# Hard-max attention on one core: dots of four query tiles per operation, and another order of the last gathers and the branch

## The chip, the core and the metric

The kernel runs on one core of one Trainium2 chip. The core has five engines that run their own instruction streams and meet at semaphores: TensorE (PE, with its weight loads as PEld), VectorE (DVE), ScalarE (ACT), GpSimd (POOL) and SyncE (SP). The metric is the device time of one execution in microseconds. Before the change it is 467.06 us, the median of three runs (467.06 to 469.16). The profile is one further execution, of 467.3 us, and its span, from the first to the last instruction, is 465.5 us.

## The reference

Attention in which the softmax is replaced by a hard maximum: every query takes the value row of the one key with the largest dot product. There are 4 batches of 4096 queries and 4096 keys, with 128 elements a row, all in fp32.

```python
def reference(q, k, v):
    logits = np.matmul(q, k.transpose(0, 2, 1))
    best = np.argmax(logits, axis=-1)
    b_idx = np.arange(q.shape[0])[:, None]
    return v[b_idx, best, :].astype(np.float32)
```

## The kernel before

**Tiles and the screen.** The queries form 128 tiles of 128, 32 a batch; `T` is 128. A tile is first screened in low precision. The 4096 keys of a batch are held as 1024 groups of 4 in a form (`kT`) from which the maximum over a group can be had by sums, differences and absolute values. For each tile, PE multiplies queries with that (`mm`, L193) and adds on the absolute values that ACT made (L202, A; added at L212). ACT evicts one half with a Relu to E (L215), DVE folds the other half from PSUM with E into packed words W (`fold`, L228), each of which also carries the number of its group, and a MAX8 takes the eight best groups of the tile (`top`, L232, into TOP).

**Candidates.** `gather` takes the best group's number out of TOP (L244, `cand`) and queues one indirect DMA for each tile, which brings three key differences of 128 elements of each query's group into a buffer `kg` (L250, issued by POOL). Before the change this is done for pairs of tiles, with eight buffers. `dots` then multiplies them with the queries on DVE (L265, `prod`), adds halves twice (L269, L272), and reduces the rest to a number (L274, `D`), again a pair at a time. `pick` compares these for chunks of eight tiles (four near the end) and forms the index of the winning key (L284 to L297: mx, near, sel, CNT, win). `put_values` queues the value gathers by that index (L304, `vr`, one a tile), and a store of four tiles on SP (L309).

**Doubtful rows.** Queries whose screen was too close to call are flagged and done exactly. This is done in two halves of the tiles. The first half is a generator (`flag_segment`) whose steps are spread over the loop's later iterations; its gathers pass through the list `fast`. The second half comes after the loop: `flags_first` and `flags_last`. There DVE and PE pack the doubtful rows' numbers together, POOL gathers their records FR, queries FQ and three candidate groups FK (`get`, L498), `exact` (L542) computes the exact products, the winners' value rows FV are gathered, and one indirect DMA scatters them to the output (L534). If there were more doubtful rows than fit, a count HARD is above zero, and `all_rows` (L571 to L593) redoes everything: all engines read that count (`hi`, L573) and branch over the block (L576). In this data the block is not entered.

**Order.** The kernel writes out the order of every engine's instructions by hand (`manual_schedule`): what is emitted first stands first in its engine's queue. The main loop (L700) runs over 128 iterations `it`. In each it emits, in this order: at most one load (`load_part`, on POOL, for a later batch), at most one piece of the transposed keys of a later batch (`unit_k`: PE, and an ACT eviction, L173), the screen of tile `it`, the fold of tile it-1, one call of `step`, MAX8 of tile it-2, the candidates of tile it-3 (`gathers`; it-2 from iteration 104 on), a second call of `step`, and `issue`. `step` lets each started generator (`dots`, `pick`, flags) go on by one piece of DVE work, with one or two `dots` pieces a call. `issue` puts key gathers (`near_q`) and value gathers (`late_q`) into POOL's queue, one of each per iteration as a rule, and two key gathers from iteration 100 on when more than two are queued. A `dots` generator waits until its gathers are in POOL's queue, then two iterations more (one from iteration 104, `TAIL`). In `yield "until", condition, n` the n is this number of iterations.

**After the loop.** The last tiles' MAX8, candidates and gathers are emitted, then the remaining `dots` and `pick`. `flags_last` mixes its steps with the value gathers that are still queued: `late(n)` emits n of them (L501: `LATE`, 8; L504: one; L525: three; L528: all that are left).

Of the kernel before, what the change touches and what calls it, by code (L numbers as in the profile page):

```python
# [10 lines left out]
U32 = mybir.dt.uint32  # L11
# [9 lines left out]
QSCALE = 128.0  # L21
TAU = 8.0
NEAR = 0.5
LATE = 8


@with_exitstack
def kernel(ctx, tc, q, k, v, out):
# [210 lines left out]
    def gather(c, t0, n):  # L239
        c0, c1 = chunks[c]  # L240
        if t0 == c0:
            cand_t[c] = sp.tile([P, c1 - c0], U32, tag=f"cand{c1 - c0}", name=f"cand_{c}", bufs=6)
        x = cand_t[c][:, t0 - c0:t0 - c0 + n]
        nc.vector.tensor_scalar(out=x, in0=TOP.bitcast(U32)[:, t0:t0 + n, 0], scalar1=IDX, scalar2=IDX,  # L244
                                op0=OP.bitwise_and, op1=OP.bitwise_xor)
        kg = rp.tile([P, n, 3, P], FP16, tag=f"kg{n}", name=f"kg_{t0}", bufs=8)
        assert len(kg_t) < 8
        kg_t[t0] = kg
        for j in range(n):
            near_q.append(lambda j=j: nc.gpsimd.indirect_dma_start(  # L250
                out=kg[:, j].rearrange("p f d -> p (f d)"), out_offset=None, in_=k16[t0 // NQT],
                in_offset=IOA(ap=x[:, j:j + 1], axis=0)))
        mark = lambda: done.add(("kg", t0))
        marks.add(mark)
        near_q.append(mark)
        start(dots(c, t0, n), "dots", c)

    def dots(c, x, m):
        c0 = chunks[c][0]
        d = D_t[c % 4]  # L260
        b = x // NQT
        yield "until", lambda: ("kg", x) in done, 1 if x >= TAIL else 2
        kg = kg_t.pop(x)
        prod = rp.tile([P, m, 3, P], FP16, tag=f"prod{m}", name=f"prod_{x}")
        nc.vector.tensor_tensor(out=prod, in0=kg, in1=natq[b % 2][:, x - b * NQT:x - b * NQT + m, :].unsqueeze(2).to_broadcast([P, m, 3, P]),  # L265
                                op=OP.mult)
        yield "dve",
        p1 = rp.tile([P, m, 3, 64], FP16, tag=f"p1{m}", name=f"p1_{x}")
        nc.vector.tensor_tensor(out=p1, in0=prod[:, :, :, 0:64], in1=prod[:, :, :, 64:128], op=OP.add)  # L269
        yield "dve",  # L270
        p2 = rp.tile([P, m, 3, 32], FP16, tag=f"p2{m}", name=f"p2_{x}")
        nc.vector.tensor_tensor(out=p2, in0=p1[:, :, :, 0:32], in1=p1[:, :, :, 32:64], op=OP.add)  # L272
        yield "dve",
        nc.vector.tensor_reduce(out=d[:, x - c0:x - c0 + m, 1:4], in_=p2, axis=AX_X, op=OP.add)  # L274
        done.add(("dot", x))

    def pick(c, t0, t1):
        n = t1 - t0
        b, qt = t0 // NQT, t0 % NQT
        d = D_t[c % 4][:, 0:n, :]  # L280
        yield "until", lambda: all(("dot", x) in done for x in range(t0, t1, 2)), 0
        cand = cand_t.pop(c)
        mx = sp.tile([P, n, 1], FP32, tag=f"mx{n}", name=f"mx_{c}")
        nc.vector.tensor_reduce(out=mx[:, :, 0], in_=d, axis=AX_X, op=OP.max)  # L284
        yield "dve",
        near = sp.tile([P, n, 4], FP32, tag=f"near{n}", name=f"near_{c}")
        nc.vector.scalar_tensor_tensor(out=near, in0=d, scalar=NEAR, in1=mx.to_broadcast([P, n, 4]),
                                       op0=OP.add, op1=OP.is_ge)
        yield "dve",
        sel = sp.tile([P, n, 4], FP32, tag=f"sel{n}", name=f"sel_{c}")  # L290
        nc.vector.tensor_tensor(out=sel, in0=near, in1=iota8.unsqueeze(1).to_broadcast([P, n, 4]), op=OP.mult)
        yield "dve",
        nc.vector.tensor_reduce(out=CNT[:, t0:t1], in_=sel, axis=AX_X, op=OP.add)
        done.add(("cnt", c))
        yield "cnt",
        win = sp.tile([P, n], U32, tag=f"win{n}", name=f"win_{c}")
        nc.vector.scalar_tensor_tensor(out=win, in0=CNT[:, t0:t1], scalar=float(b * Sk - 8), in1=cand, op0=OP.add, op1=OP.add)  # L297
        for i in range(0, n, 4):
            put_values(c, i, n, win, out[b].rearrange("(p t) d -> p t d", p=P)[:, qt + i:qt + i + 4])
# [151 lines left out]
    def flags_last(t0, t1, win_last, late):  # L451
# [45 lines left out]
        def get(dst, src, idx, hi):  # L497
            nc.gpsimd.indirect_dma_start(out=dst, out_offset=None, in_=src, in_offset=IOA(ap=idx, axis=0),  # L498
                                         bounds_check=hi - 1, oob_is_err=False)
# [22 lines left out]
        nc.vector.tensor_tensor(out=hd[:, 1:2], in0=tot[:, 1:2], in1=tot[:, 0:1], op=OP.subtract)  # L522
        for a in (hd[:, 0:1], hd[:, 1:2], tot[:, 2:3]):
            nc.vector.tensor_tensor(out=HARD, in0=HARD, in1=a, op=OP.add)
        late(3)  # L525
        win = whole(exact(FK, FQ, gb, 3, "fe"))
        get(FV, v_flat, win, B * Sk)
        late(1 << 20)  # L528
        ok = fp.tile([P, 1], FP32, tag="ok", name="ok_e")
        nc.vector.tensor_scalar(out=ok, in0=HARD, scalar1=0.5, scalar2=float(1 << 20), op0=OP.is_gt, op1=OP.mult)  # L530
        rowk = fp.tile([P, 1], U32, tag="rowk", name="rowk_e")
        nc.vector.tensor_tensor(out=rowk, in0=row, in1=ok, op=OP.add)
        all_rows()
        nc.gpsimd.indirect_dma_start(out=out_flat, out_offset=IOA(ap=rowk, axis=0), in_=FV, in_offset=None,  # L534
                                     bounds_check=P * T - 1, oob_is_err=False)

    def exact(kk, qq, grp, R, name):
        d = fp.tile([P, R, 4], FP32, tag=f"xd{R}", name=f"xd_{name}")
        for r in range(R):
            for f in range(4):  # L540
                pr = fp.tile([P, P], FP32, tag="xp", name=f"xp_{name}_{r}_{f}", bufs=2)
                nc.vector.tensor_tensor_reduce(out=pr, in0=kk[:, r, f * P:(f + 1) * P], in1=qq, scale=1.0, scalar=0.0,  # L542
                                               op0=OP.mult, op1=OP.add, accum_out=d[:, r, f:f + 1])
                yield "dve", 0.2
        ix = fp.tile([P, R, 4], FP32, tag=f"xi{R}", name=f"xi_{name}")
        nc.vector.scalar_tensor_tensor(out=ix, in0=grp.unsqueeze(2).to_broadcast([P, R, 4]), scalar=0.0,
                                       in1=iota4.unsqueeze(1).to_broadcast([P, R, 4]), op0=OP.add, op1=OP.add)
        yield "dve", 0.17
        mx = fp.tile([P, 1], FP32, tag="xm", name=f"xm_{name}")
        nc.vector.tensor_reduce(out=mx, in_=d.rearrange("p r f -> p (r f)"), axis=AX_X, op=OP.max)  # L550
        yield "dve", 0.17
        lt = fp.tile([P, R * 4], FP32, tag=f"xl{R}", name=f"xl_{name}")
        nc.vector.tensor_scalar(out=lt, in0=d.rearrange("p r f -> p (r f)"), scalar1=mx, scalar2=float(1 << 20),
                                op0=OP.is_lt, op1=OP.mult)
        yield "dve", 0.17
        nc.vector.tensor_tensor(out=lt, in0=lt, in1=ix.rearrange("p r f -> p (r f)"), op=OP.add)
        yield "dve", 0.17
        win = fp.tile([P, 1], U32, tag="xw", name=f"xw_{name}")
        nc.vector.tensor_reduce(out=win, in_=lt, axis=AX_X, op=OP.min)
        yield "dve", 0.17  # L560
        return win


    def whole(g):
        while True:
            try:
                next(g)
            except StopIteration as s:
                return s.value

    def all_rows():  # L571
        hi = fp.tile([1, 1], mybir.dt.int32, tag="hi")
        nc.vector.tensor_copy(out=hi, in_=HARD[0:1, :])  # L573
        left = nc.values_load(hi[0:1, 0:1], min_val=0, max_val=1 << 24,
                              skip_runtime_bounds_check_because="a count of rows, summed in fp32")
        with tc.If(left > 0):  # L576
# [104 lines left out]

    def gathers(t):
        for c, (t0, t1) in enumerate(chunks):
            if t0 <= t < t1 and ((t - t0) % 2 or t == t1 - 1):
                x = t0 + (t - t0) // 2 * 2
                gather(c, x, t - x + 1)
            if t == t0:
                start(pick(c, t0, t1), "pick", c)
        if t % 8 == 7:
            put_rec(t - 7, t + 1)  # L690
        if t == SEGS[1] - 1:
            last = [c for c, x in enumerate(chunks) if x[1] == t + 1][0]
            start(flag_segment(0, t + 1, lambda: ("cnt", last) in done, lambda: ("out", last) in done), "flags")
# [51 lines left out]

    screen(T)
    top(T - 2)
    fold(T - 1)
    top(T - 1)
    gathers(T - 2)  # L750
    gathers(T - 1)
    flush()
    assert not [s for s in live if s["kind"] == "flags"] and not fast
# [15 lines left out]
    for p in [s for s in live if s["kind"] == "pick"]:  # L769
        c = p["c"]  # L770
        dot = [s for s in live if s["kind"] == "dots" and s["c"] == c]
        while dot:
            two, dot = dot[:2], dot[2:]
            drain(two)
        last = c == len(chunks) - 1
        if last:
            flags_first(T // 2, T)
        drain([p], "cnt" if last else None)
    flags_last(T // 2, T, lambda: drain([p]), late_now)
    man.__exit__(None, None, None)  # L780
# [30 lines left out]
```

## Time and profile before

| | |
|---|---|
| Median of three runs | 467.06 us |
| The profiled execution, its span | 467.3 us, 465.5 us |
| Busy PE, DVE, ACT, POOL | 380.2, 417.8, 376.8, 318.1 us |
| DVE: fold W (x128), MAX8 (x128) | 166.0 us, 155.8 us busy |
| DVE: prod, p1, D, p2 (x64 each) | 34.9, 22.3, 21.5, 15.7 us busy |
| POOL: key gathers kg, value gathers vr (x128 each) | 127.4 us, 136.6 us busy |
| Key gather from issue to landing | 2.8 us, median |

Busy times of an operation in a group of rows overlap with the next operation of the same engine. The distance between the starts of two instructions that follow each other without a gap is what one of them costs its engine. The time of a DMA issue on POOL is that of the instruction that issues it; the data land later.

### The profile page before, as it was taken

The page shows a single profiled execution, that of the slowest core. Times are in us where ns is not written, and L with a number is a line of the kernel's source. Part 1 is how long each engine was busy: PE and PEld are TensorE (multiplying, and loading weights), DVE is VectorE, ACT ScalarE, POOL GpSimd, SP SyncE. Part 2 cuts the span into 40 slices and gives each one's busy share as a digit, 9 for nine tenths or more (in the row PEclk, how much of TensorE's full clock was granted, in tenths as well). Part 3 has the DMA queues.
Part 4 walks back from the last instruction along what each step waited for, and adds up shares of the span by engine and source line. Part 5 has one row for each costly group of instructions (what it writes and reads, how often), then busy time and mean ns, then how long its engine had stood idle before and what let it go on. Part 6 is the DMA issues. An engine that isn't in the chain of part 4 may idle for free.

```text
span 465.5 us, 6396 instructions
## 1 busy us (share of the span) xinstructions
PE 380.2 (82%) x1834; PEld 168.3 (36%) x1834; DVE 417.8 (90%) x825; ACT 376.8 (81%) x437; POOL 318.1 (68%) x345
## 2 busy tenths in 40 slices
PE   8999999998999889999998889998998888850100
PEld 4444444443444344444443334443333333320000
DVE  2689999999999999999999999999998999998330
ACT  2999999999999989999997889999998888840000
POOL 8233557877677888776678876677777777767730
PEclk9999999999999999999999999999999999995555
DMA  7934576853325877943235653423432333322320
GB/s 130 227 66 96 107 103 97 139 120 85 80 76 135 148 140 128 121 126 81 79 98 137 129 116 94 100 80 87 110 101 79 86 86 99 87 71 68 94 74 4
DMA packets 43624, 47.54 MB, mean 102 GB/s; under 512 B 25000, under 2 KB 33451, under 8 KB 43584
## 3 DMA queue, kind: packets, MB, share of 16 engines
q0 software_dynamic: 18752, 30.97, 33.7%
q1 hardware_dynamic: 24832, 16.13, 13.1%
q8 instruction: 14, 0.23, 0.2%
q14 instruction: 26, 0.21, 0.2%
HBM read 39.59 MB, written 12.19 MB: 111 GB/s over the span
## 4 chain that ended last, share of the span: by engine, by line
DVE 31%; issue 23%; ACT 13%; PE 13%; DMA 9%; POOL 7%; POOLq 0%; DVEq 0%; ACTq 0%
DVE W L228 14%; ACT A L202 10%; PE psn L193 5%; DVE TOP L232 5%; PE psn L212 4%; DMA kg<-k,cand 4%; ACT E L215 4%; DMA vr<-in_v_dram,win 3%; DVE prod L265 3%; PE pd L193 3%; POOL kg L250 3%; POOL vr L304 2%; DVE D L274 2%; DVE p L269 2%; DMA natk<-in_k_dram 2%
## 5 line engine op out<-in xcount | busy, mean ns | idle before, releaser
L202 ACT ACTIVATE A<-pd 128x1024 f16<-128x1024 f32 x256 | 258.6, 1041 | 23.0 <-PE pd L193 22.7
L250 POOL DMA_INDIRECT kg<-k,cand x128 | 127.4, 995 | 85.1 <-issue 26.6
L228 DVE SCALAR_TENSOR_TENSOR W<-psn,E 128x1024 int16<-128x1024 f32 x128 | 166.0, 1297 | 7.0 <-ACT E L215 5.5
L193 PE MATMUL pd<-kT,qT 128*128 128x512 f16 x512 | 151.8, 378 | 15.7 <-ACT A L202 14.8
L193 PE MATMUL psn<-kT,qT 128*128 128x512 f16 x512 | 151.8, 378 | 15.3 <-ACT A L202 7.9
L304 POOL DMA_INDIRECT vr<-in_v_dram,win x128 | 136.6, 1067 | 39.0 <-issue 37.5
L193 PEld LDWEIGHTS <-qT 128*128 128x128 f16 x1024 | 98.4, 97 | 163.9 <-issue 76.0
L232 DVE MAX8 TOP<-W 128x8 f32<-128x1024 f32 x128 | 155.8, 1217 | 0.0
L212 PE MATMUL psn<-A,identh 128*128 128x512 f16 x512 | 152.1, 378 | 0.0
L215 ACT ACTIVATE E<-psn 128x1024 int16<-128x1024 f32 x128 | 132.2, 1033 | 5.0 <-PE psn L212 5.0
L212 PEld LDWEIGHTS <-identh 128*128 128x128 f16 x512 | 49.6, 97 | 60.8
L265 DVE TENSOR_TENSOR prod<-kg,natq 128x768 f16<-128x768 f16 x64 | 34.9, 546 | 3.9 <-DMA kg<-k,cand 3.9
L269 DVE TENSOR_TENSOR p<-prod 128x384 f16<-128x384 f16 x64 | 22.3, 349 | 0.1
L274 DVE TENSOR_REDUCE D<-p 128x6 f32<-128x192 f16 x64 | 21.5, 336 | 0.1
L173 ACT ACTIVATE kT<-uk 128x256 f16<-128x256 f32 x48 | 20.1, 419 | 0.9 <-PE uk L170 0.9
L64 POOL DMA_DIRECT2D natk<-in_k_dram x27 | 16.1, 599 | 0.9 <-POOLq L795 0.8
L67 POOL DMA_DIRECT2D natq<-in_q_dram x27 | 16.3, 605 | 0.2
L169 PE MATMUL uk<-identh,natk 128*128 128x128 f16 x96 | 15.8, 218 | 0.6 <-ACT A L202 0.6
L272 DVE TENSOR_TENSOR p<-p 128x192 f16<-128x192 f16 x64 | 15.7, 245 | 0.0
L464 PE MATMUL fp_e<-n_e,tri 128*128 128x1 f32 x2 | 0.6, 361 | 16.7 <-DVE n_e L462 16.7
L170 PEld LDWEIGHTS <-natk 128*128 128x128 f16 x96 | 9.3, 97 | 7.7 <-issue 5.3
L169 PEld LDWEIGHTS <-natk 128*128 128x128 f16 x96 | 9.3, 97 | 5.6
(147 smaller groups left out, 133.5 us busy)
## 6 DMA issues: line engine op xcount, KB each, us to landing
out_dram<-vr SPq DMA_DIRECT2D x32, 256.0 KB, 2.2
natq<-in_q_dram POOLq DMA_DIRECT2D x26, 128.0 KB, 3.2
k<-kd SPq DMA_DIRECT2D x8, 384.0 KB, 4.2
natk<-in_k_dram POOLq DMA_DIRECT2D x24, 128.0 KB, 3.9
kg<-k,cand POOLq DMA_INDIRECT x128, 2.8
vr<-in_v_dram,win POOLq DMA_INDIRECT x128, 2.8
natq<-in_q_dram POOLq DMA_DIRECT2D x1, 768.0 KB
natk<-in_k_dram POOLq DMA_DIRECT2D x1, 512.0 KB, 5.2
```

What stands on the lines that cost most here:

```text
L169: nc.tensor.matmul(out=o, lhsT=natk[b % 2][:, h, 4 * m + x, :], rhs=identh, start=True, stop=False)
L193: nc.tensor.matmul(out=ps[:, n * 512:(n + 1) * 512], lhsT=qT[b % 2][:, qt * P:(qt + 1) * P], rhs=kT[b % 2][:, u * 1024 + n * 512:u * 1024 ...
L202: nc.scalar.activation(out=A, in_=ps, func=AF.Abs)
L212: nc.tensor.matmul(out=ps[:, n * 512:(n + 1) * 512], lhsT=identh, rhs=A[:, n * 512:(n + 1) * 512], start=False, stop=True)
L215: nc.scalar.activation(out=E, in_=ps, func=AF.Relu, scale=QSCALE)
L228: nc.vector.scalar_tensor_tensor(out=W_t[t % NW].bitcast(I16)[:, 1::2], in0=ps, scalar=QSCALE, in1=E, op0=OP.mult, op1=OP.max)
L232: nc.vector.max(out=TOP[:, t, :], in_=W_t[t % NW].bitcast(FP32))
L250: near_q.append(lambda j=j: nc.gpsimd.indirect_dma_start(out=kg[:, j].rearrange("p f d -> p (f d)"), out_offset=None, in_=k16[t0 // NQT], ...
L265: nc.vector.tensor_tensor(out=prod, in0=kg, in1=natq[b % 2][:, x - b * NQT:x - b * NQT + m, :].unsqueeze(2).to_broadcast([P, m, 3, P]), op ...
L269: nc.vector.tensor_tensor(out=p1, in0=prod[:, :, :, 0:64], in1=prod[:, :, :, 64:128], op=OP.add)
L274: nc.vector.tensor_reduce(out=d[:, x - c0:x - c0 + m, 1:4], in_=p2, axis=AX_X, op=OP.add)
L304: late_q.append(lambda j=j: nc.gpsimd.indirect_dma_start(out=vr[:, j, :], out_offset=None, in_=v_flat, in_offset=IOA(ap=win[:, i + j:i + j ...
```

## The change

Four things change.

- **Dots of four.** For chunks that end at tile 72 or before (`t1 <= T - 56`, which is 18 groups of four tiles), the candidates of four tiles are taken out in one operation, and p1, p2 and D are one operation for four tiles each. The product is still made in operations of two tiles. Between the pieces of such a quad stands a wait of an iteration, so that one piece falls to an iteration, and the wait after its gathers are queued is one iteration, not two. The buffers: six `kg` of four tiles for all sizes (`NKG`), where there were eight of pairs.
- **Single tiles at the end.** The last two tiles have candidates, gathers and dots of their own. Those of tile 126 are emitted ahead of the fold of tile 127. `flags_first` moves ahead of the last two tiles' dots.
- **Value gathers in the tail.** `LATE` is 7 where it was 8. After the gathers of FK all remaining value gathers are emitted, where it was three, then FV, then the rest.
- **The branch.** The copy of HARD that the branch reads, and the two small operations for the scatter's rows, come before `exact`, and `all_rows`, which holds the branch, stands ahead of the gather of FV instead of behind it. The result of `exact` has a buffer name by its size (`xw{R}`), so that the block's own `exact` has another.

The diff, cut to its core:

```diff
-LATE = 8
+LATE = 7
+NKG = 6
...
-        kg = rp.tile([P, n, 3, P], FP16, tag=f"kg{n}", name=f"kg_{t0}", bufs=8)
-        assert len(kg_t) < 8
+        kg = rp.tile([P, 4, 3, P], FP16, tag="kg", name=f"kg_{t0}", bufs=NKG)[:, 0:n]
+        assert len(kg_t) < NKG
...
-        yield "until", lambda: ("kg", x) in done, 1 if x >= TAIL else 2
+        gap = ("wait", 1) if m == 4 else ("dve",)
+        yield "until", lambda: ("kg", x) in done, 2 if m < 4 and x < TAIL else 1
         kg = kg_t.pop(x)
-        prod = rp.tile([P, m, 3, P], FP16, tag=f"prod{m}", name=f"prod_{x}")
-        nc.vector.tensor_tensor(out=prod, in0=kg, in1=natq[b % 2][:, x - b * NQT:x - b * NQT + m, :].unsqueeze(2).to_broadcast([P, m, 3, P]),
-                                op=OP.mult)
-        yield "dve",
-        p1 = rp.tile([P, m, 3, 64], FP16, tag=f"p1{m}", name=f"p1_{x}")
+        prod = rp.tile([P, 4, 3, P], FP16, tag="prod", name=f"prod_{x}")[:, 0:m]
+        h = min(m, 2)
+        for i in range(0, m, h):
+            nc.vector.tensor_tensor(out=prod[:, i:i + h], in0=kg[:, i:i + h],
+                                    in1=natq[b % 2][:, x + i - b * NQT:x + i + h - b * NQT, :].unsqueeze(2).to_broadcast([P, h, 3, P]),
+                                    op=OP.mult)
+            yield gap
+        p1 = rp.tile([P, 4, 3, 64], FP16, tag="p1", name=f"p1_{x}")[:, 0:m]
         nc.vector.tensor_tensor(out=p1, in0=prod[:, :, :, 0:64], in1=prod[:, :, :, 64:128], op=OP.add)
-        yield "dve",
-        p2 = rp.tile([P, m, 3, 32], FP16, tag=f"p2{m}", name=f"p2_{x}")
+        yield gap
+        p2 = rp.tile([P, 4, 3, 32], FP16, tag="p2", name=f"p2_{x}")[:, 0:m]
...
-        late(3)
-        win = whole(exact(FK, FQ, gb, 3, "fe"))
-        get(FV, v_flat, win, B * Sk)
         late(1 << 20)
+        hi = fp.tile([1, 1], mybir.dt.int32, tag="hi")
+        nc.vector.tensor_copy(out=hi, in_=HARD[0:1, :])
         ok = fp.tile([P, 1], FP32, tag="ok", name="ok_e")
...
-        all_rows()
+        win = whole(exact(FK, FQ, gb, 3, "fe"))
+        all_rows(hi)
+        get(FV, v_flat, win, B * Sk)
         nc.gpsimd.indirect_dma_start(out=out_flat, out_offset=IOA(ap=rowk, axis=0), in_=FV, in_offset=None,
...
     def gathers(t):
         for c, (t0, t1) in enumerate(chunks):
-            if t0 <= t < t1 and ((t - t0) % 2 or t == t1 - 1):
-                x = t0 + (t - t0) // 2 * 2
-                gather(c, x, t - x + 1)
+            m = 4 if t1 <= T - 56 else 2 if t < T - 2 else 1
+            if t0 <= t < t1 and (t - t0) % m == m - 1:
+                gather(c, t - m + 1, m)
...
     screen(T)
     top(T - 2)
+    gathers(T - 2)
+    flush()
     fold(T - 1)
     top(T - 1)
-    gathers(T - 2)
     gathers(T - 1)
     flush()
...
         while dot:
-            two, dot = dot[:2], dot[2:]
+            if last and len(dot) == 2:
+                flags_first(T // 2, T)
+            two, dot = (dot[:1], dot[1:]) if last else (dot[:2], dot[2:])
             drain(two)
-        last = c == len(chunks) - 1
-        if last:
-            flags_first(T // 2, T)
```

On the engines' queues this comes to the following. ACT's order is the same. PE's is the same but for the few matmuls of the first half's flags, which come about three iterations later, as do that half's gathers on POOL. DVE has fewer instructions, four for each quad, and five more at the end. POOL issues the same gathers and loads; a tile's key gather stands two iterations later up to tile 72, and the value gathers begin at iteration 21 where it was 18.

More of the change, by code (lines that the diff above doesn't have):

```diff
@@ L274, in dots @@
         nc.vector.tensor_reduce(out=d[:, x - c0:x - c0 + m, 1:4], in_=p2, axis=AX_X, op=OP.add)
-        done.add(("dot", x))
+        done.update(("dot", i) for i in range(x, x + m))
     def pick(c, t0, t1):
@@ L280, in pick @@
         d = D_t[c % 4][:, 0:n, :]
-        yield "until", lambda: all(("dot", x) in done for x in range(t0, t1, 2)), 0
+        yield "until", lambda: all(("dot", x) in done for x in range(t0, t1)), 0
         cand = cand_t.pop(c)
@@ L557, in exact @@
         yield "dve", 0.17
-        win = fp.tile([P, 1], U32, tag="xw", name=f"xw_{name}")
+        win = fp.tile([P, 1], U32, tag=f"xw{R}", name=f"xw_{name}")
         nc.vector.tensor_reduce(out=win, in_=lt, axis=AX_X, op=OP.min)
@@ L569, in whole, with all_rows @@
                 return s.value
-    def all_rows():
-        hi = fp.tile([1, 1], mybir.dt.int32, tag="hi")
-        nc.vector.tensor_copy(out=hi, in_=HARD[0:1, :])
+    def all_rows(hi):
         left = nc.values_load(hi[0:1, 0:1], min_val=0, max_val=1 << 24,
@@ L771 @@
         dot = [s for s in live if s["kind"] == "dots" and s["c"] == c]
+        last = c == len(chunks) - 1
         while dot:
-            two, dot = dot[:2], dot[2:]
+            if last and len(dot) == 2:
+                flags_first(T // 2, T)
+            two, dot = (dot[:1], dot[1:]) if last else (dot[:2], dot[2:])
             drain(two)
-        last = c == len(chunks) - 1
-        if last:
-            flags_first(T // 2, T)
         drain([p], "cnt" if last else None)
```

## The prediction

> **What bounds the kernel now.** I read the page first, then the table of windows, then the timelines of single engines. Busy shares and the chain's shares by engine:
>
> ```profile
> PE 380.2 (82%) x1834; PEld 168.3 (36%) x1834; DVE 417.8 (90%) x825; ACT 376.8 (81%) x437; POOL 318.1 (68%) x345
> DVE 31%; issue 23%; ACT 13%; PE 13%; DMA 9%; POOL 7%; POOLq 0%; DVEq 0%; ACTq 0%
> ```
>
> Several engines are near full, so shares of the span decide nothing. The windows (stretch; length, then busy time and count of PE, PEld, DVE, ACT, POOL; PE clock, DMA share, GB/s) do:
>
> ```profile
> 40.00:107.00 67.00, 64.68 (x320) 29.07 (x319) 67.00 (x112) 66.11 (x82) 44.48 (x50) 1.00 0.63 112
> 142.00:195.00 53.00, 48.13 (x234) 21.50 (x233) 51.23 (x88) 49.25 (x59) 42.77 (x49) 1.00 0.79 133
> 195.00:247.00 52.00, 49.60 (x244) 22.19 (x242) 52.00 (x93) 50.30 (x62) 36.56 (x37) 1.00 0.38 99
> 418.00:465.00 47.00, 1.70 (x12) 1.36 (x12) 19.18 (x92) 0.00 (x0) 23.08 (x23) 0.50 0.21 60
> ```
>
> DVE has no idle time through most of the loop, with ACT about a microsecond behind; 142–195 is the exception. DVE's timeline there and at 358 (start, busy, the idle time before in brackets):
>
> ```profile
> 192.62 0.56 DVE L265 TENSOR_TENSOR prod<-kg,natq 128x768 f16<-128x768 f16 x1 [1.06 <-DMA kg<-k,cand]
> ...
> 358.84 0.56 DVE L265 TENSOR_TENSOR prod<-kg,natq 128x768 f16<-128x768 f16 x1 [1.82 <-DMA kg<-k,cand]
> ```
>
> So time taken off DVE shortens the loop until ACT or the key gathers stand in the way. The tail is a POOL chain, in POOL's timeline:
>
> ```profile
> 435.22 0.99 POOL L498 DMA_INDIRECT FR<-rec,rr_e  x1 [0.30 <-DVE n_e L510]
> ...
> 444.37 1.00 POOL L304 DMA_INDIRECT vr<-in_v_dram,win  x1 [0.30 <-issue]
> 447.55 1.00 POOL L498 DMA_INDIRECT FV<-in_v_dram,xw_fe  x1 [2.19 <-DVE hi L573]
> 454.42 1.03 POOL L534 DMA_INDIRECT out_dram<-FV,rowk_e  x1 [5.87 <-issue]
> ```
>
> Consecutive gathers start 1.3 us apart (about 1.0 busy, 0.30 issue). The 5.87 us before the scatter is the branch, by the rows of its line:
>
> ```profile
> L576 POOLq EVENT_SEMAPHORE  x4: 17/43/1501, 449.0 to 450.7; - x4
> L576 POOLq INC_SWDGE_SEM  x1: 2410/2410/2410, 450.8 to 450.8; - x1
> ```
>
> **What the skill says.** The Trainium skill, "VectorE: DVE Perf Modes", section The TRN2 errata, gives an SBUF operation 58 cycles at 0.96 GHz on top of its elements, about 60 ns; the trace agrees (fit below: 0.06 us). "Perfetto Trace Analysis", section DMA Instruction — SWDGE (GPSIMD), says that the end of a POOL DMA in a profile is the end of descriptor generation; here it is about 1.0 us, and the page's median from issue to landing is 2.8 for kg. "Runtime: NRT & Kernel Launch", section Instruction fetch mechanics, says that a taken branch to code outside the fetched window stalls the engine; here SyncE resumes 3.0 us after its branch.
>
> **Part 1: dots of four, 18 quads.** DVE's timeline of two iterations, start to start:
>
> ```profile
> 79.55 0.32 DVE L274 TENSOR_REDUCE D<-p 128x6 f32<-128x192 f16 x1
> 79.80 1.28 DVE L228 SCALAR_TENSOR_TENSOR W<-psn,E 128x1024 int16<-128x1024 f32 x1
> 80.98 0.53 DVE L265 TENSOR_TENSOR prod<-kg,natq 128x768 f16<-128x768 f16 x1
> 81.45 1.21 DVE L232 MAX8 TOP<-W 128x8 f32<-128x1024 f32 x1
> 82.58 0.14 DVE L244 TENSOR_SCALAR cand<-TOP 128x2 uint32<-128x2 uint32 x1
> 82.64 0.34 DVE L269 TENSOR_TENSOR p<-prod 128x384 f16<-128x384 f16 x1
> 82.91 1.29 DVE L228 SCALAR_TENSOR_TENSOR W<-psn,E 128x1024 int16<-128x1024 f32 x1
> 84.10 0.23 DVE L272 TENSOR_TENSOR p<-p 128x192 f16<-128x192 f16 x1
> 84.27 1.21 DVE L232 MAX8 TOP<-W 128x8 f32<-128x1024 f32 x1
> ```
>
> The product takes 0.47, the additions 0.27 and 0.17, the reduce 0.25, cand 0.06. Product and additions lie on 0.06 us + 0.53 ns an element. Two pairs cost 2 × 1.22 = 2.43. A quad: products 2 × 0.47, p1 of 768 elements 0.47, p2 of 384 0.27, the reduce of 384 0.25 + 0.20 (192 more at 1.04 ns), one cand 0.06: 2.19. Saved 0.24, times 18: **−4.3 us**, if DVE stays the bound.
>
> Cover one, ACT. In the first tiles ACT is busy without a gap and its three evictions start 0.917 apart: 2.75 a tile, plus 0.31 for each kT eviction. In batch 0 two of those come per three iterations: 2.96. DVE there goes from 3.03 an iteration (52.26 to 103.70, 17 iterations) to 2.97, on ACT's floor. Five quads lie there, worth 1.2; I give half back: **+0.6** (bounds 0 and 1.2). Later kT evictions come every second iteration, 2.91 against some 2.98 of DVE: covered.
>
> Cover two, the gathers. A tile's gather moves from four iterations after its number to six, the first half of a quad's product reads tiles 0 and 1, and the second half an iteration later waits for tiles 2 and 3. From the quad's cand, POOL needs three rounds of gather and value gather, 3 × 2.6, plus 2.8 to land = 10.6 us; the second product comes some 5 iterations and a fold later, 15.8: slack 5. With a load in each iteration (41 to 57) a round is 3.2 to 3.3 and the landing 3.5 (median in 142–195), and lag adds up: kg of tile 36 at 136.78 to tile 51 at 186.46 is 49.7 for 15 tiles. Put behind the cand of 36–39 at 143.8, kg 51 starts at 193.5 and lands at 197.0, against its product at about 196.4 when the loop is 1 us shorter and the stall of 1.06 absent. So a stall of 0 to 0.6 takes its place: **−0.5** (bounds −1.0 and 0).
>
> **Part 2: order of the other rows.** The first flag segment's POOL rows come three iterations later (FR at 94 instead of 91). Between kg 95 and kg 105 stand 22 rows instead of 24, so kg 105 (355.06) starts up to 2.6 earlier and the wait of 1.82 goes: **−1.6** (bounds −1.8 and 0). It comes back later: six rows instead of three stand between kg 119 and kg 121, the out scatter and value gathers. kg 121 (407.86) moves to about 410.6 (3 × 1.3 less the 0.78 and some that POOL waited), lands at 413.4, for a product at 412.46: **+0.9** (bounds 0 and 3). Behind that product stand the fold, the last cands and so every later gather. kg 119 had nothing to spare (0.04), and is three rows earlier.
>
> **Part 3: tail.** One more set of four dot operations and one cand: 5 small DVE rows, mostly under the landing of kg 127 (423.09 to 425.82); the dependent chain of small operations puts mx 0.2 later. LATE 7 instead of 8 takes one value gather out from before FR: 1.3 less the 0.2 and a little waiting: FR 435.2 → 434.2, FK likewise, the exact dot products done by about 446.3. The remaining three value gathers, not two, follow FK: last at 444.6, landing 447.2. The branch's semaphore waits then end at landing, 447.3, not at FV's (450.7): −3.5. INC_SWDGE_SEM 2.41 gives 449.7; FV follows 1 us on and needs 3.1 to land, then scatter: 454.0 to 454.6 against 454.42. What was hidden behind FV's landing becomes a landing behind the branch: **+0.1** (bounds −2.4, if INC is covered by the landings, and +3.8, if the wait before it doesn't shrink).
>
> Sum: −4.3 + 0.6 − 0.5 − 1.6 + 0.9 + 0.1 = −4.8 against 467.3 of the profiled execution (span 465.5, 1.8 around it, unchanged): 462.5. The median of the runs is 467.06, 0.24 lower: **462.3**.
>
> **Rivals.** A change of 0.5%, 2.3 us, is what this measurement can tell from none: 464.7 and 469.4 are the borders.
> - **ACT or gathers take the savings** (0.18): of the 4.3 only 1.5 remains, and of the 1.6 at 358 only 0.4, since another kg wait takes its place: 467.06 − 1.5 − 0.4 + 0.9 = 466.1. For: ACT's 66.11 of 67.00. Against: ACT's floor binds in one batch alone.
> - **FV's round trip stays bare** (0.10): reordering the branch doesn't do what it says; 462.3 + 3.8 = 466.1. For: its landing now starts after the branch. Against: the 1.50 us wait at the branch was for FV.
> - **The branch's increment is hidden** (0.10): 462.3 − 2.4, and without the stall at 412: 459.0.
> - **Slower: quads' gathers late** (0.17). Place: the second product of each quad. If gathers land some 6 us after issue, as the one for 192.62 did (186.46 plus 6.08), and POOL doesn't run ahead within a quad, DVE stops at every quad. A mean stall of 0.5 gives 462.3 + 9 = 471.3; it decides from 0.4 (18 × 0.4 = 7.2 over 462.3 passes 469.4). Against: slack 5, median 2.8.
>
> **Chances and range.** The forecast holds 0.45, with its own range 460.3 to 464.7. Faster: 0.45 + 0.10 = 0.55. Same: 0.18 + 0.10 = 0.28. Slower: 0.17. The range 459.5 to 470.5 leaves out some 0.05 below (half of the hidden increment) and 0.10 above (over half of the slower case), the bounds of ACT, stalls and tail inside it.
>
> **What would show it.** p1 of 768 at 0.47 and the reduce of 384 at 0.45, start to start; DVE without gaps in 40–107, or gaps released by ACT or psn; no kg wait over 0.6 at quads' second products; nothing before the product of tiles 104–105, some 0.9 before that of 120–121; FR a microsecond earlier against kg 127; the branch's waits ending at the last value gather's landing, INC still 2.4, FV after it and 3.1 bare before the scatter. Wrong would make it: ACT gaps in all batches, kg waits at every quad, or an FV that starts later than 451.

## The result and the profile after

The changed kernel takes **462.37 us** (median of four runs, 461.14 to 462.96) where the kernel before takes 467.06. The ratio is 0.9888, with a 95% interval of 0.9858 to 0.9919: about 1.1% faster. The forecast was 462.3. That the sum met the time is partly luck: several of its terms were off, and their errors cancelled, as is shown below.

The profiled execution of the changed kernel took 462.96 us, with a span of 461.1 against 465.5, 4.4 us less. Its page gives for busy time and counts:

```profile
PE 380.2 (82%) x1834; PEld 168.1 (36%) x1834; DVE 414.6 (90%) x758; ACT 376.3 (82%) x437; POOL 314.3 (68%) x345
```

DVE has 67 instructions fewer. The windows, with the same stretches and columns as before:

```profile
40.00:107.00 67.00, 65.50 (x328) 29.67 (x327) 66.12 (x89) 67.00 (x83) 39.40 (x46) 1.00 0.60 109
142.00:195.00 53.00, 50.21 (x248) 22.54 (x247) 51.60 (x75) 51.22 (x62) 42.97 (x48) 1.00 0.74 133
195.00:247.00 52.00, 48.99 (x240) 21.86 (x239) 52.00 (x77) 49.72 (x61) 39.22 (x40) 1.00 0.41 100
418.00:465.00 47.00, 1.71 (x12) 1.37 (x12) 17.14 (x93) 0.00 (x0) 20.35 (x20) 0.52 0.19 56
```

In 40–107 the two engines have changed places: ACT is now busy all the time, DVE has 0.88 us of idle time. In 195–247 DVE is still full. A quad on DVE looks like this (timeline; start, duration, operation):

```profile
68.47 0.35 DVE L277 TENSOR_TENSOR p<-p 128x384 f16<-128x384 f16 x1
68.73 1.23 DVE L233 MAX8 TOP<-W 128x8 f32<-128x1024 f32 x1
69.87 0.15 DVE L245 TENSOR_SCALAR cand<-TOP 128x4 uint32<-128x4 uint32 x1
69.92 0.55 DVE L279 TENSOR_REDUCE D<-p 128x12 f32<-128x384 f16 x1
70.39 1.30 DVE L229 SCALAR_TENSOR_TENSOR W<-psn,E 128x1024 int16<-128x1024 f32 x1
...
77.60 0.55 DVE L274 TENSOR_TENSOR p<-prod 128x768 f16<-128x768 f16 x1
78.07 1.22 DVE L233 MAX8 TOP<-W 128x8 f32<-128x1024 f32 x1
```

From start to start: p1 of 768 elements 0.47, p2 of 384 0.26, the reduce of 384 0.47. All waits of DVE that are longer than 0.2 us between 36 and 425 us:

```profile
39.84 1.31 DVE L229 SCALAR_TENSOR_TENSOR W<-psn,E 128x1024 int16<-128x1024 f32 x1 [0.79 <-ACT E L216]
48.69 1.31 DVE L229 SCALAR_TENSOR_TENSOR W<-psn,E 128x1024 int16<-128x1024 f32 x1 [0.28 <-ACT E L216]
52.16 1.30 DVE L229 SCALAR_TENSOR_TENSOR W<-psn,E 128x1024 int16<-128x1024 f32 x1 [0.59 <-issue]
194.79 0.56 DVE L269 TENSOR_TENSOR prod<-kg,natq 128x768 f16<-128x768 f16 x1 [1.40 <-DMA kg<-k,cand]
360.34 0.56 DVE L269 TENSOR_TENSOR prod<-kg,natq 128x768 f16<-128x768 f16 x1 [0.28 <-DMA kg<-k,cand]
408.89 0.56 DVE L269 TENSOR_TENSOR prod<-kg,natq 128x768 f16<-128x768 f16 x1 [1.31 <-DMA kg<-k,cand]
```

The first three fall in a stretch in which DVE has hardly any dots yet and ACT is busy without a pause (14.00 of 14.00 us in 39 to 53, where DVE is busy 12.32 us, against 13.98 before the change). Two of them end with ACT's eviction E; what ended the third the profile does not name. The three waits for key gathers are those at tiles 50–51, 106–107 and 120–121. Before the change DVE waited at some other places, for PE:

```profile
174.88 1.31 DVE L228 SCALAR_TENSOR_TENSOR W<-psn,E 128x1024 int16<-128x1024 f32 x1 [0.32 <-PE psn L212]
181.23 1.31 DVE L228 SCALAR_TENSOR_TENSOR W<-psn,E 128x1024 int16<-128x1024 f32 x1 [0.40 <-PE psn L212]
277.16 1.31 DVE L228 SCALAR_TENSOR_TENSOR W<-psn,E 128x1024 int16<-128x1024 f32 x1 [0.22 <-PE psn L212]
```

And the tail, in POOL's timeline and by the rows of the branch's line:

```profile
430.70 0.99 POOL L503 DMA_INDIRECT FR<-rec,rr_e  x1 [0.98 <-DVE tb_e L496]
...
441.23 1.07 POOL L309 DMA_INDIRECT vr<-in_v_dram,win  x1 [0.30 <-DMA FK<-in_k_dram,gb_e]
447.27 0.99 POOL L503 DMA_INDIRECT FV<-in_v_dram,xw_fe  x1 [4.96 <-DVEq L580]
450.01 1.03 POOL L540 DMA_INDIRECT out_dram<-FV,rowk_e  x1 [1.75 <-DMA FV<-in_v_dram,xw_fe]
```

```profile
L580 POOLq EVENT_SEMAPHORE  x4: 17/43/2319, 438.3 to 441.6; - x4
L580 DVEq COMPARE_BRANCH  x1: 72/72/72, 443.6 to 443.6; - x1
L580 POOLq INC_SWDGE_SEM  x1: 2390/2390/2390, 444.0 to 444.0; - x1
L580 DVEq EVENT_SEMAPHORE  x1: 21/21/21, 446.6 to 446.6; - x1
```

The branch waits 2.32 us for the last value gather (441.6 to 443.9), the row INC_SWDGE_SEM, called the increment here, takes 2.39, FV starts about 0.9 after that, and the scatter follows FV by 2.74. Scatter to end of span is 11.1 us in every profile of this study.

Cutting both traces at the same instructions (folds of tiles 0, 58, 61 and 126, the scatter) puts the gain in place. Figures are differences of start times in the timelines.

| stretch | before | after | difference |
|---|---|---|---|
| fold 0 to fold 58 | 178.12 | 172.42 | -5.70 |
| fold 58 to fold 61 | 8.62 | 10.29 | +1.67 |
| fold 61 to fold 126 | 211.43 | 211.70 | +0.27 |
| fold 126 to scatter | 39.81 | 38.96 | -0.85 |

The wait for the gather of tile 51 lies in the first stretch before the change and in the second after it. All of the loop's gain shows in the first half. Part of it is only work put off, because the dots of tiles stand some iterations later there and are caught up after tile 79: the lead is 6.9 us at the fold of tile 80 and 4.8 at that of tile 84.

### The profile page after: what moved, and what is told of

It is laid out like the page before. It is cut to its first block, busy times and chain, and to the rows that moved or that the text cites. A ratio compares the mean times of both kernels' runs of the same rounds, so it can differ in the third digit from the quotient of the medians.

```text
span 461.1 us, 6319 instructions
## 1 busy us (share of the span) xinstructions
PE 380.2 (82%) x1834; PEld 168.1 (36%) x1834; DVE 414.6 (90%) x758; ACT 376.3 (82%) x437; POOL 314.3 (68%) x345
## 5 line engine op out<-in xcount | busy, mean ns | idle before, releaser
L251 POOL DMA_INDIRECT kg<-k,cand x128 | 125.7, 982 | 80.5 <-DVE cand L245 45.2
L309 POOL DMA_INDIRECT vr<-in_v_dram,win x128 | 134.7, 1053 | 40.3 <-issue 35.6
L269 DVE TENSOR_TENSOR prod<-kg,natq 128x768 f16<-128x768 f16 (+1 forms) x65 | 35.3, 543 | 3.0 <-DMA kg<-k,cand 3.0
L174 ACT ACTIVATE kT<-uk 128x256 f16<-128x256 f32 x48 | 20.4, 424 | 1.4 <-PE uk L171 1.4
L274 DVE TENSOR_TENSOR p<-prod 128x384 f16<-128x384 f16 (+2 forms) x47 | 20.0, 426 | 0.1
L279 DVE TENSOR_REDUCE D<-p 128x6 f32<-128x192 f16 (+2 forms) x47 | 19.7, 419 | 0.1
L277 DVE TENSOR_TENSOR p<-p 128x192 f16<-128x192 f16 (+2 forms) x47 | 13.5, 287 | 0.1
```

The source lines that it names most:

```text
L174: nc.scalar.activation(out=kT[b % 2][:, c:c + 256], in_=ps, func=AF.Copy)
L251: near_q.append(lambda j=j: nc.gpsimd.indirect_dma_start(out=kg[:, j].rearrange("p f d -> p (f d)"), out_offset=None, in_=k16[t0 // NQT], ...
L269: nc.vector.tensor_tensor(out=prod[:, i:i + h], in0=kg[:, i:i + h], in1=natq[b % 2][:, x + i - b * NQT:x + i + h - b * NQT, :].unsqueeze(2 ...
L309: late_q.append(lambda j=j: nc.gpsimd.indirect_dma_start(out=vr[:, j, :], out_offset=None, in_=v_flat, in_offset=IOA(ap=win[:, i + j:i + j ...
```

## Experiments

Each kernel differs from the changed one by the diff shown, cut to its core where dots stand. Times are medians, ratios are to the kernel before, run beside it. They ran on three chips: the first four kernels below on one, the next four (LATE 8 to quads that wait two iterations) on a second, the last four on a third. The kernel before took 466.84, 466.90 and 466.60 us there.

**The changed kernel again.**

> The changed kernel once more, beside the variants, as their yardstick. Theory: 462.0 to 462.9 as before, ratio 0.988 to 0.991. A rival that the earlier median was a lucky chip would show 463.5 or more.

462.53 us, 0.9907 (0.9883 to 0.9930), as its theory said; the rival of a lucky chip is out. This is the yardstick of the next three, which ran on the same chip. Where later kernels are compared with it, that is across chips.

**Quads alone.** Everything from the last two tiles on as before the change.

```diff
-LATE = 7
+LATE = 8
...
+        late(3)
+        win = whole(exact(FK, FQ, gb, 3, "fe"))
+        get(FV, v_flat, win, B * Sk)
         late(1 << 20)
...
-        win = whole(exact(FK, FQ, gb, 3, "fe"))
...
         all_rows(hi)
-        get(FV, v_flat, win, B * Sk)
...
-            m = 4 if t1 <= T - 56 else 2 if t < T - 2 else 1
+            m = 4 if t1 <= T - 56 else 2
...
```

> Quads alone: dots of four up to tile 72 as in the changed kernel, everything from the last two tiles on as before (a pair of last gathers, LATE 8, FV ahead of the branch). Theory: the loop's gain at the fold of tile 120, 5.2 us in the changed kernel, comes whole, the stall of about 1.4 at the product of tiles 120 and 121 too, and the tail's 0.85 is missing: 463.0 to 463.8. Rival, that the tail carries the gain: 466 or more.

463.15 us, 0.9934 (0.9907 to 0.9961), as the theory said. In the trace fold 126 to scatter is 39.77, the 39.81 of before.

**Tail alone.**

```diff
-NKG = 6
+NKG = 8
-            m = 4 if t1 <= T - 56 else 2 if t < T - 2 else 1
+            m = 2 if t < T - 2 else 1
```

> Tail alone: dots of pairs up to tile 125 as before (eight buffers), single last gathers, LATE 7 and the branch ahead of FV as in the changed kernel. Theory: only the tail's 0.85 us is gained, or less where POOL is late at the end: 466.0 to 467.0. Rival, that the tail carries the gain: 463 to 464.5.

466.07 us, 0.9977 (0.9962 to 0.9992); fold 126 to scatter is 38.91. The two halves, 3.7 and 0.8 us against the 466.84 that the kernel before took on this chip, make 4.5 where the whole makes 4.3: the quads are the larger part by far, and the rival that the tail carries the gain is out. By its median the tail's part is small against the spread of the runs, but it stands in the traces: fold 126 to scatter is 39.8 in both profiles without the new tail, and 38.9 to 39.0 in six with it and an unchanged order of the rows before it.

**FV ahead of the branch again.**

```diff
-        all_rows(hi)
         get(FV, v_flat, win, B * Sk)
+        all_rows(hi)
```

> The changed kernel with one swap back: the gather of FV ahead of the branch again; the copy of HARD and the rest stay early. Theory: moving the branch is worth next to nothing, since one landing of 2.7 to 3.1 us stands before the branch's increment of 2.4 either way (FV's before, the last value gather's after): FV starts at about 443.5, lands at 446.4, increment to 448.8, scatter about 449.9 against 450.01, so within 0.5 us of the changed kernel. Rival, that the branch's place is what shortened the tail: 2 to 3 us longer than the changed kernel.

462.27 us, 0.9904 (0.9880 to 0.9928): no difference to the yardstick. POOL's timeline and the branch's increment in that kernel:

```profile
442.15 0.99 POOL L503 DMA_INDIRECT FV<-in_v_dram,xw_fe  x1 [0.89 <-DVE xw_fe L565]
448.94 1.03 POOL L540 DMA_INDIRECT out_dram<-FV,rowk_e  x1 [5.79 <-issue]
```

```profile
L580 POOLq INC_SWDGE_SEM  x1: 2410/2410/2410, 445.4 to 445.4; - x1
```

FV goes out 4.0 us earlier (32.1 us after fold 126 against 36.1), but now the branch waits for its landing, and the scatter comes after the increment. FR to scatter is 19.24 us here and 19.28 in the yardstick. Moving the branch ahead of FV is worth nothing where it stands: one landing lies before the increment in either order.

**Where the tail's gain is, then.** Three more kernels, with parts of the tail changed.

LATE 8 alone (`-LATE = 7`, `+LATE = 8`):

> The changed kernel with LATE 8 alone. Theory: POOL's increment comes 1.0 earlier, but FR and so the exact products come 0.3 later, and DVE resumes 3.0 us after its branch, which now ends last: FV within 0.3 us of the changed kernel's place, 462.2 to 462.8. Rival, that POOL's increment alone sets FV: 461.5.

462.57 us, 0.9901 (0.9883 to 0.9918).

LATE 8 and the branch ahead of the exact products:

```diff
-LATE = 7
+LATE = 8
-        win = whole(exact(FK, FQ, gb, 3, "fe"))
         all_rows(hi)
+        win = whole(exact(FK, FQ, gb, 3, "fe"))
```

> The changed kernel with the branch still earlier in DVE's and SP's order (ahead of the exact products) and LATE 8. Theory: with LATE 8 POOL's 0.98 us of idle time before FR is filled, so the last value gather and the branch's increment come 1.0 earlier, and DVE's pause behind its branch (3.0 us) hides in its wait for FK: 461.3 to 461.9 where the changed kernel has 462.5. Rival, that FV waits for the exact products: no change.

461.53 us, 0.9882 (0.9864 to 0.9900).

The last two tiles as a pair again:

```diff
-            m = 4 if t1 <= T - 56 else 2 if t < T - 2 else 1
+            m = 4 if t1 <= T - 56 else 2
...
-    gathers(T - 2)
-    flush()
     fold(T - 1)
     top(T - 1)
+    gathers(T - 2)
     gathers(T - 1)
...
```

> The changed kernel with the last two tiles as a pair again (their gathers behind the fold of tile 127, four dot operations instead of eight, LATE 7 and the branch as changed). Theory: the pair waits for its gathers by 0.9 us and then needs two operations fewer than the singles, a net of some 0.3 on the small operations before FR, of which POOL's idle time before FR covers nothing: 462.3 to 462.8. Rival, that the single last gathers carry the tail's gain: 463.2.

462.16 us, 0.9884 (0.9859 to 0.9910), 0.1 below the theory's range and far from the rival. The single tiles bring nothing; by the trace the tail is 38.95 with the pair and 38.96 with singles. (In this kernel `flags_first` also stands behind the dots of both tiles again.) A pair waits 0.95 us for its gathers, and singles have four more operations.

The times of the first two of these came as the theory had them, but the theory of LATE 8 is refuted by its trace. It said that FV would be held by DVE, which resumes 3.0 us after its branch. In that kernel FV starts before DVE has resumed:

```profile
446.76 0.99 POOL L503 DMA_INDIRECT FV<-in_v_dram,xw_fe  x1 [5.07 <-DMA FK<-in_k_dram,gb_e]
```

```profile
L580 POOLq INC_SWDGE_SEM  x1: 2390/2390/2390, 443.5 to 443.5; - x1
L580 DVEq EVENT_SEMAPHORE  x1: 21/21/21, 447.1 to 447.1; - x1
```

FV starts about 0.9 after the increment's end in the changed kernel and in both kernels with LATE 8, so POOL's own branch sets it. Counted from the fold of tile 126, the start of FV goes from 36.1 or 36.2 (LATE 7) to 35.5 (LATE 8) and 35.4 (LATE 8 and early branch): LATE 8 gains 0.6, and the early branch next to nothing. The scatter follows at 39.0, 38.6 and 38.2, because FV took 3.1 us to it in the second and 2.8 in the third. So of the 1.0 between the medians of the two kernels with LATE 8, the tails explain 0.4 at most. In the profile of LATE 8 the wait at tiles 50–51 was the longest of all:

```profile
195.10 0.56 DVE L269 TENSOR_TENSOR prod<-kg,natq 128x768 f16<-128x768 f16 x1 [1.82 <-DMA kg<-k,cand]
```

That wait differs among profiles though no instruction ahead of it differs: under 0.2 in three of them (all on the third chip, where a fourth has 1.39), 0.47 to 1.82 in the other kernels with quads and their wait of one iteration. With pairs it differs as well: 1.06 in the kernel before, and under 0.2 with the tail alone. Medians of these kernels should not be read closer than a microsecond.

So, by the traces, the tail's 0.8 us has two sources that stand in for each other. With FV ahead of the branch, FV waits for the exact products, and LATE 7 brings those forward (FR 20.4 us after fold 126 with quads alone, 19.7 with FV first). With the branch ahead of FV, the increment waits for the last value gather, and the exact products have 4 us to spare. Undoing one source alone costs nothing. (LATE 7 by itself, in an otherwise old tail, was not run.)

**Quads that wait two iterations.**

```diff
-        yield "until", lambda: ("kg", x) in done, 2 if m < 4 and x < TAIL else 1
+        yield "until", lambda: ("kg", x) in done, 2 if x < TAIL else 1
```

> The changed kernel with quads waiting two iterations after their gathers are in POOL's queue, not one. Theory: the stall of 0.5 to 1.4 us at the second product of tiles 48 to 51 goes, since the gathers have 2.9 us more; DVE comes that much earlier to the last iterations, where POOL is without a pause: 461.5 to 462.5. Rival, that POOL holds the stretch by its number of rows: the stall moves to another wait in the same stretch, 462.5.

463.38 us, 0.9920 (0.9904 to 0.9936): 0.9 longer than the yardstick, which neither theory nor rival had. The wait at tiles 50–51 is gone, as expected, and fold 0 to fold 61 is 1.4 us shorter. But fold 61 to 126 is 1.3 longer and fold 126 to scatter 1.1 longer. The trace points to a row of the first half's doubtful rows, in POOL's timeline:

```profile
299.19 0.94 POOL L251 DMA_INDIRECT kg<-k,cand  x1 [0.30 <-issue]
304.75 1.00 POOL L420 DMA_INDIRECT FR<-rec,rr  x1 [4.62 <-issue]
306.06 1.01 POOL L309 DMA_INDIRECT vr<-in_v_dram,win  x1 [0.30 <-issue]
308.35 1.12 POOL L251 DMA_INDIRECT kg<-k,cand  x1 [1.29 <-issue]
```

FR stands in POOL's queue before its row numbers are ready, and the key gathers behind it wait with it; 0.99 and 0.69 of waits follow at tiles 104–107. In the changed kernel FR waits 3.85 at the same place, which prompted the following.

**FR one iteration later.**

```diff
+        yield "wait", 1
         get(FR, rec, rr, P * T)
         get(FQ, q_flat, row, P * T)
         yield "until", lambda: not fast, 3
```

> The changed kernel with the first half's flag gathers one iteration later: FR enters POOL's queue at iteration 95, not 94, when its row numbers are ready. Theory: POOL's wait of 3.85 us at 302 us falls to under 1, POOL runs 3 us earlier from there, the stall of 1.4 us at tiles 120 and 121 and the 0.35 at 360 us go, and what remains is DVE's own chain: 460.7 to 461.3. Rival, the row order alone makes that stall: 0.8 or more of it stays, 462.2.

461.94 us, 0.9894 (0.9875 to 0.9912), short of the theory; nor does the stall stay, as the rival had it. POOL did not keep the lead:

```profile
300.96 1.01 POOL L420 DMA_INDIRECT FR<-rec,rr  x1 [1.35 <-issue]
304.09 1.00 POOL L309 DMA_INDIRECT vr<-in_v_dram,win  x1 [2.12 <-issue]
```

The wait at FR was mostly time in which the rows behind it would have waited too: the value gather behind it now waits 2.12. The stall at tiles 120–121 did go, because the scatter of the first half moved behind the gather of tile 121. From fold 61 to the scatter this profile needs 250.3 us and the yardstick's 250.6, so almost nothing of it reached the end: fold 61 to 126 is 1.2 shorter, and the tail 0.9 longer. The quads that wait two iterations have the same two signs, no stall at tiles 120–121 with the scatter behind the gather of tile 121, and FR as late in the tail (20.86 us after fold 126 in both, 19.67 in the yardstick), although FR waited 4.62 there. So their longer tail is not shown to be the price of that wait; it goes with the row that moved.

**Two value gathers out of the way of tile 121.**

```diff
-LATE = 7
+LATE = 9
-        take_late(2 if n == 0 and len(late_q) > 4 or it >= T - 24 and it % 2 == 0 else 1)
+        if it not in (122, 123):
+            take_late(2 if n == 0 and len(late_q) > 4 or it >= T - 24 and it % 2 == 0 else 1)
+        elif it == 122:
+            take_late(1)
```

> The changed kernel with two value gathers taken out from before the gather of tile 121 (iterations 122 and 123) and given back before FR (LATE 9). The stall of 1.4 us at the product of tiles 120 and 121 should go either way. Theory that POOL's rows set the end: the two gathers, 2.6 us, stand before FR instead, and nothing is gained: 462.2 to 463.0. Rival, the row order between tiles 119 and 121 alone costs the 0.9 of the prediction: 461.1 to 461.7.

461.11 us, 0.9875 (0.9855 to 0.9894), in the range of the rival, the row order. The stall of 1.4 is gone, fold 61 to the scatter is 249.0 us against 250.6, and the last value gather stands as far behind fold 126 as in the yardstick (30.1 us). FR comes 2.6 us later after fold 126, but the exact products had that to spare. The rows come out even because POOL's idle times of 0.76 (before the gather of tile 124) and 0.98 (before FR) are filled now; both rows start 0.30 after the end of the one ahead of them:

```profile
412.29 0.95 POOL L251 DMA_INDIRECT kg<-k,cand  x1 [0.30 <-issue]
430.51 1.00 POOL L503 DMA_INDIRECT FR<-rec,rr_e  x1 [0.30 <-issue]
```

The last value gather stands 36.4 us behind the gather of tile 121, where it was 35.2 in the yardstick: the two rows moved cost 1.2 behind the stall, and not 2.6. So the stall does cost what it lasts, if the rows moved find idle time of POOL behind it. In the kernel with the later FR the same two idle times are filled, but the scatter that moved waits 0.93 itself, and the last value gather stands 36.5 us behind the gather of tile 121: that one row cost the whole 1.3. This is the fastest kernel of the study by its median, but it ran on another chip than the yardstick, and their intervals overlap.

**Both ideas together** (FR later, branch ahead of the exact products, LATE 8, a pair at the end):

```diff
+        yield "wait", 1
         get(FR, rec, rr, P * T)
...
-LATE = 7
+LATE = 8
...
+        all_rows(hi)
         win = whole(exact(FK, FQ, gb, 3, "fe"))
-        all_rows(hi)
...
-            m = 4 if t1 <= T - 56 else 2 if t < T - 2 else 1
+            m = 4 if t1 <= T - 56 else 2
```

> The same with the branch ahead of the exact products, LATE 8 and the last two tiles as a pair. Theory: the gains of the later FR (1.4) and of the earlier branch with LATE 8 (1.0) add up: 459.6 to 460.6. Rival, that both draw on the same idle time of POOL before the second half's FR: 460.7 to 461.5.

461.61 us, 0.9887 (0.9869 to 0.9906): 1.0 above the theory's range and 0.1 above the rival's. The gains of 1.4 and 1.0 that the theory added were not there to add. From fold 61 to the scatter the profiles are shorter than the yardstick's by 0.3 (later FR), 0.5 (LATE 8 and early branch) and 1.0 us (both). Whether such small gains add up, the runs do not settle. That both draw on POOL's idle time before FR fits: it is 0.98 in the yardstick and 0.30 with the later FR alone.

**Quads to tile 95.**

```diff
-            m = 4 if t1 <= T - 56 else 2 if t < T - 2 else 1
+            m = 4 if t1 <= T - 32 else 2 if t < T - 2 else 1
```

> The changed kernel with quads up to tile 95 instead of tile 71: six more. Theory that POOL bounds the loop from 302 us on (its row FR waits 3.85 us for the rows of the doubtful queries, and then POOL works without a pause to 413 us): DVE's 6 x 0.24 = 1.4 us are not gained, 462.0 to 463.2, and the chunks' results come later. Rival, that DVE bounds it all the way: 461.1.

463.92 us, 0.9938 (0.9917 to 0.9959), 0.7 above even the theory's range. DVE does gain the 1.4: fold 0 to fold 104 is 1.8 us shorter than in the yardstick, and to fold 108 still 1.0. Then one gather takes it all back:

```profile
353.85 0.56 DVE L269 TENSOR_TENSOR prod<-kg,natq 128x768 f16<-128x768 f16 x1 [2.39 <-DMA kg<-k,cand]
```

That is the product of tiles 104 and 105, behind the rows of the doubtful queries. POOL has no idle time over 0.31 from 302 to 413 us, as the theory had it, though FR waits only 0.30 in this kernel. So tile 72 as the limit is not a matter of DVE, with this order of POOL's rows.

## Why the prediction was right, step by step

- **The bound.** DVE was the bound of the loop, and time taken off it shortened the loop. Right; quads alone give 3.7 us of 4.3.
- **Quads, -4.3.** Right in mechanism, slightly small. From fold 16 to fold 32, with no waits in either kernel, four quads save 47.83 - 46.78 = 1.05 us, 0.26 each, 4.7 for 18.
- **ACT, +0.6 in the stretch of five quads.** Wrong in place. In that stretch the saving is the same 0.26 a quad as later. The loss stands ahead of it: the first quad's product comes at iteration 11 instead of 8, so DVE has too little to fill iterations 9 to 13 with, and waits 0.79 + 0.28 + 0.59 = 1.66 us, where the kernel before has no wait over 0.2. This cause is read from the trace; no kernel with pairs in the first tiles and quads behind them was run. The quads that wait two iterations bear it out at one place: their first product comes an iteration later, and the fold that it stood ahead of waits 0.77 instead of 0.28, by about the 0.47 of a product. The step costed how long DVE's work is, and not when the first of it can start.
- **Key gathers in iterations 41 to 57, -0.5.** Before: 1.06, and 0.32 and 0.40 of PE waits near it; after: 1.40. Net -0.4, though the stall was put at 0 to 0.6. That the term came out is luck: this wait goes from under 0.2 to 1.82 among profiles, and the term left the PE waits out. The gather was issued at 191.17, as worked out (193.5 less the 2.3 us by which the loop was ahead), and its landing of 3.6 is the 3.5 assumed. DVE came to it early; the PE waits ahead of it had gone too.
- **Tiles 104–105, -1.6.** 1.82 there became nothing there and 0.28 at the next product: -1.5.
- **Tiles 120–121, +0.9.** 1.31, from the rows named; the deferral of two value gathers takes it away.
- **Tail, +0.1.** Measured -0.85. The order of FV and branch is worth nothing, as forecast; the last value gather, its landing and the increment came within 0.4 us of the working. Mis-sized was the end: FV to scatter was taken as 3.1 us of landing and 0.2 to 0.8 more, and is 2.74 in all.

Sum of the measured terms: -4.7 + 1.66 - 0.4 - 1.5 + 1.3 - 0.85, and a PE wait of 0.22 near 277 us that went, make -4.7; the span shows -4.4, with 0.2 of it a later first fold. The start cost 1.1 more than forecast and the stall at tiles 120–121 0.4 more; the quads gave 0.4 more and the tail 0.9 more. These cancel.

Of the rivals, ACT as a bound came true for some iterations only, and the late quads at one quad out of 18. FV's round trip does lie bare, 2.74 us of it, but the wait ahead of the increment became shorter as worked out, so the 3.8 of that rival did not come. A hidden increment can be excluded: it takes 2.39 on the path.

## What to carry to other kernels

When an engine's small operations are merged, ask when the first merged one can start as well as how much each saves; a pipeline that fills later idles at its start, here by 1.66 us. Reordering a wait and a transfer gains only if the number of transfers that must land one after another falls: count the landings on the path in both orders. And a row moved past a stall pays only if idle time behind the stall takes up what was moved.

## What was not expected of the hardware

- The same key gather (tile 51, in iteration 57), after the same instructions, made DVE wait from under 0.2 to 1.82 us, from one profile to the next, in a stretch where the DMA engines are busy 0.74 of the time (in the changed kernel's profile). What decides it was not tried.
- An engine that took the branch resumes 2.8 to 3.0 us later in the changed kernel (DVE 443.6 to 446.6, SyncE 445.0 to 447.8), and 2.5 to 4.0 us later in the other profiles. The Trainium skill, "Runtime: NRT & Kernel Launch", section Instruction fetch mechanics, says that a taken branch out of the fetched window has to fetch by DMA; the traces agree with such a pause, but do not show what fills it. On POOL the increment lies in its place: it takes 2.39 to 2.41 us in all 14 profiles, and starts when the last gather that POOL issued before it has landed (the last value gather's in the changed kernel, FV's where FV stands ahead of the branch). FV follows about 0.9 us after it.
